# Where weight slabs and the tiles multiplied with them begin in SBUF, by remainder by 256 bytes

## The chip, the cores and the metric

The kernel runs on one core of a Trainium2 chip. The metric is the device time of one execution in microseconds; of several runs the median counts. The time before is 2227.2 us, the median of 3 runs (2226.93 to 2227.43).

## The reference

Two blocks follow each other on 256 tokens of width 1024, all in float32. The first block is one layer of attention with three branches, a pooling mixer and an MLP of width 4096 with a squared ReLU. The second block has two layers: sliding-window attention and a gated short convolution, each followed by a layer of experts. The experts take most of the time:

```python
def peer_ffn(xn, w_query, sub_keys, expert_u, expert_v):
    ...
    s_top, i_top = lax.top_k(s, PEER_TOPK)
    ...
    g = jax.nn.softmax(g_s, axis=-1)
    ...
        u = jnp.take(expert_u, ic, axis=0)
        a = jnp.einsum('td,thkd->thk', xc, u).astype(jnp.float32)
        w = (gc * jax.nn.gelu(a, approximate=False)).astype(xc.dtype)
        v = jnp.take(expert_v, ic, axis=0)
        return jnp.einsum('thk,thkd->td', w, v)
```

There are 16384 experts per layer. The kernel does not gather: it multiplies all tokens with all rows of `expert_u`, sets the weight of those that a token did not choose to zero, and multiplies with all rows of `expert_v`.

## The kernel before

**Slabs.** All weights come from HBM as 715 slabs of 128 partitions x 1024 float32 values (512 KB), in the order of one list, `plan`. The class `Stream` loads a slab into one of three raw places (`wraw`, a DMA on SP's queue), and then splits it: ScalarE rounds it to a high part `wh` (float32r, L70), and VectorE, or GpSimd for some slabs, subtracts to get the low part `wl` (L71). There are four places for `wh` and four for `wl`; slab j uses place j modulo 4 of each. `W.get()` gives the next slab and sees to it that the three after it are being split.

**Products.** The activations are kept in two parts too. A product is three matmuls into the same PSUM bank, written in `dense3`: high weights by high activations, high weights by low activations, low weights by high activations.

```python
        mm(out, h[:, s], xh[:, 0, k], first and opens, False)
        mm(out, h[:, s], xh[:, 1, k], False, False)
        mm(out, l[:, s], xh[:, 0, k], False, last)
```

All matmuls go through the helper `mm` (L174). In most stages (`tmode`) a block of the slab, 128 columns, is the weight operand that TensorE loads, and a tile of activations, 256 columns (one for each token), is the moving operand. These tiles are `xh` (two of them, used in turn by most stages), `mid` (the hidden values of the MLP, 4 tiles), `xo` and `oh` (attention outputs), `ph` and `mh` (pooling mixer) and `gA` (the convolution's tile takes this place). In the second half of each expert layer (`mix`) it is the other way round: a block of `xh` (the weighted activations) is the weight operand, and half of a slab part, 512 columns, is the moving operand; its results are in the banks named `g`. Two small products have narrow weights: `gh` (24 columns, blocks 96 bytes apart, by `xh`) and `movh` (30 columns, by slab parts).

**Order.** Each expert layer is written out in a manual order. While TensorE multiplies with `expert_u`, VectorE chooses the top 16 for each token and head (`topk`) and then builds one-hot tables, from which TensorE makes the gates (`gate`). Both are cut into pieces, and after each slab's matmuls some pieces follow, by fixed costs. The order of all instructions is therefore set when the program is built.

**Where tiles begin.** Tiles are taken from pools, and a pool hands out the bytes of a partition one after another. Where a tile begins follows from what was asked for ahead of it. A slice of a slab part that is loaded as weights begins at a multiple of 512 bytes from the part's start, and a moving slice of activations at a multiple of 1024, so each has the remainder by 256 of its tile.

Of the kernel before, what the change touches and what calls it, by code (L numbers as in the profile page):

```python
# [8 lines left out]
F32 = mybir.dt.float32  # L9
F32R = mybir.dt.float32r  # L10
# [8 lines left out]
P = 128  # L19
# [28 lines left out]
class Stream:  # L48
# [11 lines left out]
    def pump(self, i):  # L60
        nc, n = self.nc, len(self.plan)
        while True:
            if self.split < min(i + self.AHEAD + 1, n) and self.split < self.loaded:
                j = self.split
                self.split += 1
                r = self.raw.pop(j)
                h = self.pool.tile([P, 1024], F32R, name="wh", bufs=self.SPL)
                l = self.pool.tile([P, 1024], F32R, name="wl", bufs=self.SPL)
                for s in (slice(0, 1024),) if j else (slice(0, 512), slice(512, 1024)):
                    nc.scalar.copy(h[:, s], r[:, s])  # L70
                    (nc.gpsimd if j in self.pooled else nc.vector).tensor_sub(l[:, s], r[:, s], h[:, s].bitcast(F32))  # L71
                self.hl[j] = (h, l)
            elif self.loaded < n and self.loaded < self.split + self.RAW:
                self.load()
            else:
                return

    def load(self, half=None):

        if half != 1:  # L80
            self.raw[self.loaded] = self.pool.tile([P, 1024], F32, name="wraw", bufs=self.RAW)
            self.loaded += 1
        j = self.loaded - 1
        s = slice(0, 1024) if half is None else slice(512 * half, 512 * half + 512)
        self.nc.sync.dma_start(self.raw[j][:, s], self.plan[j][:, s])
# [21 lines left out]
def build(tc, a):  # L107
# [172 lines left out]
    xhp = ctx.enter_context(tc.tile_pool(name="xhp", bufs=1))  # L280

    def xh_tile(i):
        return xhp.tile([P, 2, KD, T], F32R, name=f"xh{i}")

    def sq_tile():
        return glob.tile([P, KD, T], F32, name="misc")
# [19 lines left out]
    bp = b1.enter_context(tc.tile_pool(name="b1", bufs=1))  # L306
    pa = b1.enter_context(tc.tile_pool(name="pa", bufs=1, space=PSUM))

    xh = xh_tile(0)
    sq = sq_tile()  # L310
    for i in range(0, KD, 2):
# [81 lines left out]
    for u in range(2):  # L393
        h, l = W.get()
# [24 lines left out]
    for c in range(2):  # L419
        for u in range(4):  # L420
            wh, wl = W.get()
# [229 lines left out]
    h, l = W.get()  # L651
# [54 lines left out]
    ff = ExitStack()  # L706
    fpool = ff.enter_context(tc.tile_pool(name="ff", bufs=1))
    pf = ff.enter_context(tc.tile_pool(name="pf", bufs=1, space=PSUM))
    mid = [fpool.tile([P, 2, KD, T], F32R, name=f"mid{i}") for i in range(4)]
    rel = [fpool.tile([P, 2, T], F32, name=f"rel{i}") for i in range(2)]  # L710
    sq2 = fpool.tile([P, 2, T], F32, name="sq2")
# [232 lines left out]
    for u in range(2):  # L944
        h, l = W.get()
# [552 lines left out]
```

## Time and profile before

| | us |
|---|---|
| median of 3 runs | 2227.2 |
| lowest and highest of them | 2226.93, 2227.43 |
| the profiled execution's own time | 2228.21 |
| its span, first to last instruction | 2226.4 |
| TensorE busy in the span | 2186.1 |
| VectorE busy | 1594.8 |
| ScalarE busy | 1084.5 |
| GpSimd busy | 148.2 |

The profile is of one execution. Matmuls are pipelined: the recorded duration of one is longer than the distance to the next, so durations in a row overlap, and the sum of a group's durations is more than the time it takes. The load of a matmul's weights is recorded as an instruction of its own (PEld), and runs beside the matmul ahead of it. L174 is the line of the helper, so groups are told apart by the names of their tiles: `mm<-xh,wh` is a matmul into a bank named mm with `xh` and `wh` as its two operands.

### The profile page before, as it was taken

To read this page: it belongs to the slowest core of one execution; us is meant where nothing else is said; L and a number is where in the kernel's file an instruction comes from. 1 tells how busy PE (TensorE), PEld (TensorE's weight loads), DVE (VectorE), ACT (ScalarE), POOL (GpSimd) and SP (SyncE) were. 2 spreads that over 40 slices of the span, in tenths; PEclk is the share of its full clock that TensorE was granted. 3 is DMA by queue.
4 is the path that set the end of the run, shared out by engine and by line. 5 is a ranking of instruction groups with operands and counts; after the bars stand their busy time and mean duration, and the time that the engine had idled before them with its cause. 6 is when DMAs were issued, how large, how long until landed. Compare 5 with 4: busy or idle time off the path is not lost.

```text
span 2226.4 us, 39574 instructions
## 1 busy us (share of the span) xinstructions
PE 2186.1 (98%) x15892; PEld 2040.8 (92%) x15892; DVE 1594.8 (72%) x2802; ACT 1084.5 (49%) x1707; POOL 148.2 (7%) x66
## 2 busy tenths in 40 slices
PE   8999999999989999999999999999899999999999
PEld 7899999999989999988888889999899999888887
DVE  7757656666998899755555566779988986555555
ACT  5555555564434444445454454544444435454454
POOL 0000000001442000000000000044300000000000
PEclk9999999999999999999999999999999999999999
DMA  6435555334544444455555555545444445555554
GB/s 208 152 133 180 181 190 190 105 134 151 189 143 167 152 161 157 164 196 190 197 190 196 191 172 180 191 164 174 154 150 162 152 147 195 197 191 196 191 190 150
DMA packets 105625, 382.67 MB, mean 172 GB/s; under 512 B 11985, under 2 KB 12385, under 8 KB 105185
## 3 DMA queue, kind: packets, MB, share of 16 engines
q1 hardware_dynamic: 105120, 378.04, 48.9%
q8 instruction: 124, 2.03, 0.4%
q0 software_dynamic: 320, 2.11, 0.3%
q14 instruction: 61, 0.49, 0.1%
HBM read 379.05 MB, written 1.05 MB: 171 GB/s over the span
## 4 chain that ended last, share of the span: by engine, by line
PE 84%; DVE 10%; issue 3%; ACT 2%; DMA 1%; SPq 0%; ACTq 0%; DVEq 0%
PE mm L174 46%; PE g L174 34%; DVE wl L71 3%; PE s L174 2%; DVE gA L1117 2%; ACT wh L70 1%; PE o L174 1%; DVE gA L1115 1%; DVE gA L1114 1%; DMA wraw<-in_w_in 0%; DVE gA L1197 0%; DVE lows L1178 0%; DVE misc L1179 0%; DMA x<-in_x 0%; DVE gA L1087 0%
## 5 line engine op out<-in xcount | busy, mean ns | idle before, releaser
L71 DVE TENSOR_TENSOR wl<-wraw,wh 128x1024 fp32r<-128x1024 f32 (+1 forms) x660 | 824.0, 1249 | 512.5 <-ACT wh L70 509.1
L174 PE MATMUL mm<-xh,wh 128*128 128x256 f32 x6240 | 1148.6, 286 | 9.1 <-ACT wh L70 6.9
L70 ACT CAST wh<-wraw 128x1024 fp32r<-128x1024 f32 (+1 forms) x716 | 747.0, 1054 | 726.3 <-PE g L174 332.6
L174 PEld LDWEIGHTS mm<-xh,wh 128*128 128x128 f32 x6240 | 979.9, 193 | 11.7 <-ACT wh L70 7.5
L174 PE MATMUL mm<-xh,wl 128*128 128x256 f32 x3120 | 889.1, 285 | 13.2 <-DVE wl L71 13.2
L174 PE MATMUL g<-wh,xh 128*128 128x512 f32 x2048 | 632.6, 389 | 0.0
L174 PEld LDWEIGHTS mm<-xh,wl 128*128 128x128 f32 x3120 | 602.4, 193 | 15.5 <-DVE wl L71 15.4
L174 PEld LDWEIGHTS g<-wh,xh 128*128 128x128 f32 x2048 | 384.4, 188 | 79.8
L174 PE MATMUL g<-wl,xh 128*128 128x512 f32 x1024 | 398.4, 389 | 0.0
L174 PEld LDWEIGHTS g<-wl,xh 128*128 128x128 f32 x1024 | 192.2, 188 | 39.5
L71 POOL TENSOR_TENSOR wl<-wraw,wh 128x1024 fp32r<-128x1024 f32 x56 | 142.7, 2547 | 285.2 <-ACT wh L70 271.5
L1199 ACT ACTIVATE gA<-g 128x96 f32<-128x96 f32 (+14 forms) x72 | 23.4, 343 | 243.8 <-DVE gA L1197 225.2
L1218 DVE TENSOR_TENSOR xh<-gA,xh 128x256 fp32r<-128x256 f32 x224 | 93.5, 418 | 0.0
L1217 ACT CAST xh<-gA 128x256 fp32r<-128x256 f32 x224 | 90.1, 403 | 0.0
L174 PE MATMUL mm<-mid,wh 128*128 128x256 f32 x512 | 87.1, 276 | 0.0
L1234 ACT ACTIVATE gA<-mm 128x512 f32<-128x512 f32 (+15 forms) x112 | 55.6, 496 | 63.4 <-PE mm L174 63.4
L174 PEld LDWEIGHTS mm<-mid,wh 128*128 128x128 f32 x512 | 77.0, 188 | 0.0
L174 PE MATMUL g<-misc 128*128 128x128 f16 x512 | 67.0, 221 | 9.9 <-DVE misc L1179 9.9
L174 PEld LDWEIGHTS <-misc 128*128 128x128 f16 x1024 | 59.8, 98 | 13.1 <-issue 6.8
L174 PE MATMUL mm<-mid,wl 128*128 128x256 f32 x256 | 70.7, 276 | 0.0
L174 PE MATMUL g<-lows,misc 128*128 128x128 f16 x512 | 66.4, 220 | 0.0
L1197 DVE SCALAR_TENSOR_TENSOR gA<-g,gA 128x512 f32<-128x512 f32 (+30 forms) x114 | 57.1, 538 | 0.0
(346 smaller groups left out, 1570.2 us busy)
## 6 DMA issues: line engine op xcount, KB each, us to landing
wraw<-in_peer_u SPq DMA_DIRECT2D x256, 512.0 KB, 3.5
wraw<-in_peer_v SPq DMA_DIRECT2D x256, 512.0 KB, 3.5
wraw<-in_w_ff SPq DMA_DIRECT2D x64, 512.0 KB, 4.4
wraw<-in_w_query SPq DMA_DIRECT2D x32, 512.0 KB, 3.6
wraw<-in_w_in SPq DMA_DIRECT2D x29, 512.0 KB, 4.0
wraw<-in_w_cin SPq DMA_DIRECT2D x24, 512.0 KB, 3.6
wraw<-in_w_qkv SPq DMA_DIRECT2D x12, 512.0 KB, 4.1
wraw<-in_w SPq DMA_DIRECT2D x8, 512.0 KB, 3.5
```

The costliest lines, as they stand in the source:

```text
L70: nc.scalar.copy(h[:, s], r[:, s])
L71: (nc.gpsimd if j in self.pooled else nc.vector).tensor_sub(l[:, s], r[:, s], h[:, s].bitcast(F32))
L174: PE.matmul(out, l, r, start=start, stop=stop, skip_group_check=True)
L1114: V.tensor_tensor(eq, pb, J[:, None].to_broadcast([P, 2, NCAND, 16]), op=OP.is_equal)
L1115: V.tensor_tensor(prod, eq, code[:, hq:hq + 2, :, None].to_broadcast([P, 2, NCAND, 16]), op=OP.mult)
L1117: V.reduce_sum(sel[:, hq:hq + 2], prod.rearrange("p h c k -> p h k c"), axis=AX.X)
L1197: V.scalar_tensor_tensor(v, pr[:, i0:j], 2.0 ** -15, v, op0=OP.mult, op1=OP.mult)
L1199: S.activation(d[:, j - i0:i1 - i0, t0:t0 + 8], pr[:, j:i1], AF.Copy, scale=2.0 ** -15)
L1217: S.copy(w[0], gA(e))
L1218: V.tensor_sub(w[1], gA(e), w[0].bitcast(F32))
L1234: S.activation(d[:, :, n:], ps[:, :, n:], AF.Gelu)
```

## The change

The change moves tiles by inserting small unused ones. Ahead of the first tile of each of the eight places of slab parts 32 bytes are taken, and the eight places become tiles with names of their own (`wh0`, `wl0`, `wh1` and so on), each used by every fourth slab, as before. Ahead of `xh` 32 bytes are taken, and ahead of `mid` 64.

```diff
-                h = self.pool.tile([P, 1024], F32R, name="wh", bufs=self.SPL)
-                l = self.pool.tile([P, 1024], F32R, name="wl", bufs=self.SPL)
+                h, l = self.place("wh", j), self.place("wl", j)
...
+    def place(self, name, j):
+
+        name = f"{name}{j % self.SPL}"
+        if j < self.SPL:
+            self.pool.tile([P, 8], F32, name="gap" + name)
+        return self.pool.tile([P, 1024], F32R, name=name)
...
+    xhp.tile([P, 8], F32, name="gap")
     xh = xh_tile(0)
...
+    fpool.tile([P, 16], F32, name="gap3")
     mid = [fpool.tile([P, 2, KD, T], F32R, name=f"mid{i}") for i in range(4)]
```

In the two built programs the tiles begin at these bytes of a partition (remainder by 256 behind each):

| tile | before | after |
|---|---|---|
| `wh`, four places | 35808, 39904, 44000, 48096 (all 224) | 35840 (0), 44096 (64), 52352 (128), 60608 (192) |
| `wl`, four places | 52192, 56288, 60384, 64480 (all 224) | 39968 (32), 48224 (96), 56480 (160), 64736 (224) |
| `wraw`, three places | 13280, 17376, 21472 (all 224) | the same |
| `xh`, two tiles | 68576, 84960 (both 224) | 68864, 85248 (both 0) |
| `mid`, four tiles | 112544 and every 16384 after it (all 160) | 112896 and every 16384 after it (all 0) |
| `xo`, `gA` | 142048, 150240; 101856 (all 224) | 142336, 150528; 102144 (all 0) |
| `oh`, `ph`, `mh` | 148736, 177664, 185856 (all 0) | 149024, 177952, 186144 (all 32) |

The instructions of every engine, their order and what they wait for are the same in the two programs.

## Rows read from the trace of the kernel before

**Rows 1.** The page: busy time of each engine, share of the span, instructions.

```profile
PE 2186.1 (98%) x15892; PEld 2040.8 (92%) x15892; DVE 1594.8 (72%) x2802; ACT 1084.5 (49%) x1707; POOL 148.2 (7%) x66
```

**Rows 2.** The page: the chain that ended last, by engine and by line.

```profile
PE 84%; DVE 10%; issue 3%; ACT 2%; DMA 1%; SPq 0%; ACTq 0%; DVEq 0%
PE mm L174 46%; PE g L174 34%; DVE wl L71 3%; PE s L174 2%; DVE gA L1117 2%; ACT wh L70 1%; PE o L174 1%; DVE gA L1115 1%; DVE gA L1114 1%; DMA wraw<-in_w_in 0%; DVE gA L1197 0%; DVE lows L1178 0%; DVE misc L1179 0%; DMA x<-in_x 0%; DVE gA L1087 0%
```

**Rows 3.** Three stretches: PE, PEld, DVE, ACT, POOL busy us; clock, DMA share, GB/s.

```profile
600.00:707.00 107.00, 98.04 (x797) 97.28 (x797) 103.78 (x192) 44.87 (x52) 44.50 (x17) 0.97 0.45 157
707.00:886.00 179.00, 179.00 (x1687) 177.88 (x1687) 155.55 (x230) 79.67 (x163) 0.00 (x0) 0.99 0.45 158
1515.00:1622.00 107.00, 98.01 (x805) 97.22 (x804) 103.80 (x198) 45.40 (x53) 44.71 (x17) 0.98 0.46 158
```

**Rows 4.** The chain in order of time, three pieces: start, us, what, how many.

```profile
309.93 72.43 PE mm L174 x639
...
918.48 37.48 PE mm L174 x312
...
955.96 345.47 PE g L174 x1524
```

**Rows 5.** TensorE by shape, 918 to 955 us: count | busy us, mean ns.

```profile
L174 PE MATMUL mm<-xh,wh 128*128 128x256 f32 x204 | 36.8, 283 | 0.0
L174 PE MATMUL mm<-xh,wl 128*128 128x256 f32 x102 | 28.9, 283 | 0.0
```

**Rows 6.** TensorE by shape, 310 to 390 us.

```profile
L174 PE MATMUL mm<-mid,wh 128*128 128x256 f32 x426 | 72.5, 276 | 0.0
L174 PE MATMUL mm<-mid,wl 128*128 128x256 f32 x213 | 58.8, 276 | 0.0
```

**Rows 7.** TensorE by shape, 166 to 180 us.

```profile
L174 PE MATMUL mm<-oh,wh 128*128 128x256 f32 x64 | 11.4, 279 | 0.0
L174 PE MATMUL mm<-oh,wl 128*128 128x256 f32 x32 | 9.0, 281 | 0.0
```

**Rows 8.** Groups by shape, whole run: matmuls (PE) and weight loads (PEld).

```profile
L174 PE MATMUL mm<-xh,wh 128*128 128x256 f32 x6240 | 1148.6, 286 | 9.1 <-ACT wh L70 6.9 <-ACT gA L1234 0.7 <-ACT xh L195 0.6
L174 PEld LDWEIGHTS mm<-xh,wh 128*128 128x128 f32 x6240 | 979.9, 193 | 11.7 <-ACT wh L70 7.5 <-ACT xh L195 0.9 <-DVE xh L196 0.9
L174 PE MATMUL mm<-xh,wl 128*128 128x256 f32 x3120 | 889.1, 285 | 13.2 <-DVE wl L71 13.2
L174 PE MATMUL g<-wh,xh 128*128 128x512 f32 x2048 | 632.6, 389 | 0.0
L174 PE MATMUL g<-wl,xh 128*128 128x512 f32 x1024 | 398.4, 389 | 0.0
L174 PE MATMUL mm<-mid,wh 128*128 128x256 f32 x512 | 87.1, 276 | 0.0
L174 PEld LDWEIGHTS mm<-mid,wh 128*128 128x128 f32 x512 | 77.0, 188 | 0.0
L174 PE MATMUL mm<-mid,wl 128*128 128x256 f32 x256 | 70.7, 276 | 0.0
```

**Rows 9.** TensorE by shape, 600 to 707 us, then 1515 to 1622 us.

```profile
L174 PE MATMUL mm<-xh,wh 128*128 128x256 f32 x518 | 95.7, 287 | 0.0
L174 PE MATMUL mm<-xh,wl 128*128 128x256 f32 x259 | 74.6, 288 | 5.7 <-DVE wl L71 5.7
...
L174 PE MATMUL mm<-xh,wh 128*128 128x256 f32 x523 | 96.2, 286 | 0.0
L174 PE MATMUL mm<-xh,wl 128*128 128x256 f32 x262 | 75.3, 287 | 5.6 <-DVE wl L71 5.6
```

**Rows 10.** The tiles gh and movh: count, duration ns min/median/max, first and last start.

```profile
L174 PE MATMUL mm<-xh,gh x24: 276/278/679, 45.7 to 48.8; 128*24 128x256 f32 x24
...
L174 PE MATMUL o<-wh,movh x64: 276/277/284, 48.9 to 59.7; 128*30 128x256 f32 x64
```

**Rows 11.** TensorE by shape, 955.7 to 957.3 us.

```profile
L174 PE MATMUL g<-wh,xh 128*128 128x512 f32 x5 | 1.6, 392 | 0.0
```

## The prediction

> **What bounds the kernel.** I read the page's busy times first, then the chain of waits, then a table by stage, then the groups of TensorE by shape. TensorE is busy in 98% of the span [rows 1], and the chain that ended last lies on it for 84%, on the matmuls of slab parts above all [rows 2]. Two places are different: while the top-k runs in each of the two expert layers (600 to 707 us and 1515 to 1622 us), VectorE is busy in 103.78 of 107 us and TensorE waits for it [rows 3]. In the stretch after it, 707 to 886 us, VectorE has 155.55 of 179 us [rows 3], so it could follow a TensorE that is some per cent faster; the granted clock is 0.97 to 0.99 in all three. So the time is a number of matmuls times their distance from each other, outside of 2 x 107 us.
>
> **How a distance is read.** 312 matmuls of `xh` by slab parts take 37.48 us, which is 120.1 ns each; 639 of `mid` by slab parts take 72.43 us, 113.3 ns each; 1524 of 512 columns take 345.47 us, 226.7 ns each [rows 4]. In the same stretches the recorded durations are 283, 276 and 389 ns [rows 5, 6, 8]. Each is 163 ns more than the distance, so for matmuls in a row a duration less 163 is the distance. That lets single groups be read where the chain merges them.
>
> **The row that this change is about.** The 283 and the 276 belong to the same instruction: 128x128 weights, 256 moving columns, the same three products (high part twice, low part once) for each block. What differs is where the operands lie. With `xh` both operands have remainder 224 by 256; with `mid` the weights have 224 and the moving tile 160, a difference of +64. With `oh` (weights 224, moving 0, a difference of -32) the durations are 279 (high) and 281 (low), so (2x279+281)/3-163 = 117 ns [rows 7]. The load of the next weights is recorded beside the running matmul, and its own mean is 193 ns with `xh` and 188 ns with `mid` [rows 8]. So the distance seems to hang on where the weight load reads against the moving read: 120 at difference 0, 117 at -32, 113 at +64.
>
> **The change part by part.**
> 1. Instructions, DMAs, waits and their order: nothing is added, removed or moved on any queue. A place is used again by every fourth slab, as before, so no new wait arises. Cost 0.
> 2. The 256-column matmuls of `xh`. There are 6240 + 3120 = 9360 [rows 8]. Those in the two VectorE-bound stretches, 518+259+523+262 = 1562 [rows 9], gain nothing: there VectorE's work sets the pace. That leaves 7798. Before, all stand at difference 0. After, the slab parts stand at 0, 64, 128, 192 (high) and 32, 96, 160, 224 (low) against moving tiles at 0. The rows know three of these eight with full weights: 120, 113, 117. All eight occur in the small product with `gh` (24 columns of weights, blocks 96 bytes apart): durations from 276, median 278, so 115 ns; the product with `movh` (30 columns), at many more differences, has 276 to 284 and a median of 277, 114 ns [rows 10]. Short loads read less and should collide less. I take 116 ns, between those 115 and the mean of 120, 113 and 117. The ends are 113.3 (all clear) and 120 (none better); no row of steady matmuls is above that. Gain: 7798 x 4.0 ns = 31.2 us, ends 0 and 7798 x 6.7 = 52.2 us.
> 3. The 768 matmuls with `mid` (512 + 256) [rows 8] already stand at 113.3. Their tile moves to remainder 0 and meets the same mix as the others, 116: a loss of 768 x 2.7 = 2.1 us, ends 0 and 768 x 6.7 = 5.1.
> 4. The 512-column matmuls (2048 + 1024) [rows 8], where the slab part is the moving operand. Difference 0 before, the mix after. Two readings of 226.7. As 389-283 = 106 ns for 256 more columns, it could be those 120 and undisturbed columns after that; then the same 6.7 ns of collision is in it, and clear ones would be at 220. Or it is 2 x 113.3, as clear as `mid`, and can only get worse: right after the stage begins, five matmuls have a mean of 392, 3 ns more than later [rows 11], so these do settle into a better state. I weigh the first reading higher, since the weight load ends long before 512 columns have passed, and take half of its 4 ns: 3072 x 2.0 = 6.1 us gain; ends 3072 x 6.7 = 20.6 gain, and 3072 x 3 = 9.2 loss.
> 5. The few hundred with `xo`, `gA`, `oh`, `mh` and `ph` and the short ones: under 2 us in either direction, taken as 0.
> 6. The splits on ScalarE and VectorE read and write the moved places too. They are hidden: VectorE has 72% [rows 1] and its waits are not on the chain but for the two stretches. No row tells what a remainder does to them; I take 0, and 2% of the 208 us in the two stretches [rows 3], 4 us, as a bound both ways.
>
> Sum: 31.2 - 2.1 + 6.1 = 35.2 us gain. The profiled execution took 2228.2 us (span 2226.4), so 2193 for it. The median of the runs, 2227.2, is 1.0 below it, so I predict **2192 us**. What is late next: the split of slabs on VectorE in the 707 to 886 us stretch, still with a few per cent to spare, and the slab DMAs, whose engines have a busy share of 0.45 to 0.46 in these stretches [rows 3].
>
> **A rule that speaks against it.** The rows show 120 and 113 for one instruction. The Trainium skill, SBUF — State Buffer, section Who interferes with whom, gives TensorE two independent read ports, one for the moving operand and one for the weights, and says "PE and ACT never wait on anyone". By that rule the places would change nothing and the sum would be 0. The trace speaks against it with 283 beside 276, but each of the two belongs to its own stage, so it isn't settled; it is rival C.
>
> **The rivals.** (About 0.2%, 4.5 us, is what a measurement of this kernel can tell from no change.)
> - A, nearly everything clears: 256 columns at 114 or less, 512 columns near 220. 7798 x 6 + 3072 x 4 to all ends = 59 to 73 us gain, so 2154 to 2168. For: five of the eight differences are unseen with full weights, and the one at +64 is perfectly clear. Against: even with narrow weights, `gh` and `movh` have medians 1 and 2 ns above the clear 276 and single rows far above it [rows 10].
> - B, little clears: what matters is only that some difference exists which isn't +64; all go as `oh`, 117 to 118. 7798 x 2.2 = 17.2, less 768 x 4.5 = 3.5 for `mid`: 13.7 gain, about 2213.
> - C, no effect of places: `mid` is faster for a reason of its stage, and 2227 stays. Against: `oh` and `mh` are in the middle of stages with `xh`, with the same slabs, the same engines at work, and still differ.
> - D, slower: the 512-column matmuls lose the settled state. Place: both weighted sums, 3072 matmuls. Price: 3 ns each, 9.2 us, and 5.1 us for `mid` at 120. It decides when the 7798 gain less than 1.3 ns each (9.2+5.1-4.5 = 9.8 us over 7798). With 0.5 ns: 14.3 - 3.9 = 10.4 us slower, 2238. For: the rows at the stage's start are longer; at a difference that changes from slab to slab it could start anew each time. Against: short loads and `oh` show that 256-column matmuls gain at nearly every other difference.
>
> **Chances and range.** The forecast (2180 to 2205) 0.54, A 0.17, B 0.15, C 0.08, D 0.06. Faster by over 0.2%: 0.54+0.17+0.15 = 0.86. Within: 0.08. Slower: 0.06. The range leaves out D, C and the outer third of A, 0.06+0.08+0.06 = 0.20: from 2160 to 2222.
>
> **What would show it.** Right: the duration of `xh` by slab parts in the steady stretch falls from 283 to about 279, not evenly, but with a pattern that repeats every four slabs; `mid` rises from 276 to about 279; the two stretches of top-k keep their 107 us; the 512-column group is at or a little under 389. Wrong: all four places alike (then the difference isn't what counts), `mid` still at 276 (then the stage is what counts), the 512-column group over 389 (D), or a gain of TensorE that comes back as idle time before `wl` L71.

## The result, and the profile after

The changed kernel takes 2240.36 us in the median of 3 runs (2239.64 to 2240.98), against 2227.2 before: the ratio is 1.0059, 95% interval 1.0036 to 1.0082. It is 13 us slower, where 35 us faster was forecast. The profiled execution after took 2240.98 us, with a span of 2239.2.

First the page after: busy times, and the chain that ended last by engine and by line (L180 is now the line of the matmul helper, L69 and L70 the two splits).

```profile
PE 2192.3 (98%) x15892; PEld 2029.2 (91%) x15892; DVE 1595.0 (71%) x2802; ACT 1083.9 (48%) x1707; POOL 149.9 (7%) x66
...
PE 74%; DVE 15%; ACT 5%; issue 4%; DMA 2%; POOL 0%; SPq 0%; ACTq 0%; DVEq 0%
```

TensorE is still busy in 98% of the span, with the same number of instructions on every engine as in [rows 1]; its share of the chain went from 84% [rows 2] to 74%, VectorE's from 10 to 15.

Next the groups of TensorE by shape, whole run, after (count | busy us, mean ns | idle before).

```profile
L180 PE MATMUL mm<-xh,wh 128*128 128x256 f32 x6240 | 1132.4, 283 | 12.0 <-ACT wh L69 6.3 <-ACT gA L1242 4.3 <-DVE mh L202 0.5
L180 PE MATMUL mm<-xh,wl 128*128 128x256 f32 x3120 | 884.6, 284 | 15.4 <-DVE wl L70 15.1
L180 PE MATMUL g<-wh,xh 128*128 128x512 f32 x2048 | 641.8, 393 | 0.0
L180 PE MATMUL g<-wl,xh 128*128 128x512 f32 x1024 | 405.5, 396 | 0.0
L180 PE MATMUL mm<-mid,wh 128*128 128x256 f32 x512 | 90.8, 280 | 0.0
L180 PE MATMUL mm<-mid,wl 128*128 128x256 f32 x256 | 72.1, 281 | 0.0
```

Against [rows 8]: `xh` fell from 286 and 285 to 283 and 284, `mid` rose from 276 to 280 and 281, and the 512-column matmuls rose from 389 to 393 and 396. The chain in order of time says it in distances (start, us, what, how many):

```profile
917.92 36.90 PE mm L180 x312
954.82 353.69 PE g L180 x1524
```

The row of 312 `xh` matmuls is 0.58 us shorter than in [rows 4] (118.3 ns each for 120.1), the row of 1524 with 512 columns 8.22 us longer (232.1 for 226.7).

How single matmuls spread is seen in the view of one tile's instructions (count: duration ns min/median/max, first and last start). Before, 1100 to 1108 us:

```profile
L174 PE MATMUL g<-wh,xh x25: 389/389/389, 1099.8 to 1107.9; 128*128 128x512 f32 x25
L174 PE MATMUL g<-wl,xh x12: 389/389/389, 1100.2 to 1107.7; 128*128 128x512 f32 x12
```

and after, the same stretch:

```profile
L180 PE MATMUL g<-wh,xh x24: 388/393/398, 1099.9 to 1107.8; 128*128 128x512 f32 x24
L180 PE MATMUL g<-wl,xh x12: 390/398/401, 1099.7 to 1107.4; 128*128 128x512 f32 x12
```

Before, every one of them takes 389 ns; after, they take from 388 to 401, and 34 of the 36 take more than 389. The `xh` matmuls in 920 to 930 us spread likewise, around a lower median. Before, then after:

```profile
L174 PE MATMUL mm<-xh,wh x58: 283/283/283, 919.8 to 930.0; 128*128 128x256 f32 x58
L174 PE MATMUL mm<-xh,wl x28: 283/283/283, 920.0 to 929.8; 128*128 128x256 f32 x28
```

```profile
L180 PE MATMUL mm<-xh,wh x58: 276/280/286, 919.9 to 930.0; 128*128 128x256 f32 x58
L180 PE MATMUL mm<-xh,wl x29: 276/281/286, 919.8 to 929.7; 128*128 128x256 f32 x29
```

**Where the 13 us came from.** The two programs issue the same 15,892 matmuls in the same order, so each can be paired with itself in the other trace, and the distance to the next start compared. "Without a wait" is a distance under 315 ns in both traces. Summed by kind, after less before:

| distances after | matmuls | us |
|---|---|---|
| 512 columns | 3071 | +16.4 |
| `mid` | 768 | +3.7 |
| `xh`, slab parts, outside the two top-k stretches, without a wait | 7783 | -12.8 |
| the two top-k stretches, waits and all | 1597 | +0.7 |
| everything else, without a wait | 2610 | +0.2 |
| waits outside of them | 62 | +4.7 |
| sum | 15891 | +12.9 |

The sum is the difference of the spans, 2239.2 less 2226.4. Per matmul that is -1.6 ns for `xh`, +4.8 for `mid`, +5.3 for 512 columns. Of the 7783 `xh` distances, 7561 are steady ones (under 140 ns in both traces), and their mean fell from 119.9 to 118.0 ns; the other 222, longer ones, took 1.7 us more. Two rows show where part of the `xh` gain came back. The top-k stretch did not move with TensorE (PE, PEld, DVE, ACT, POOL busy us; clock; DMA share; GB/s):

```profile
600.00:707.00 107.00, 95.92 (x799) 94.81 (x798) 103.86 (x192) 44.79 (x52) 44.77 (x17) 0.98 0.47 158
707.00:883.00 176.00, 176.00 (x1691) 174.90 (x1690) 152.62 (x226) 79.42 (x163) 0.00 (x0) 1.00 0.48 158
```

VectorE has 103.86 us of the 107, as in [rows 3], and TensorE idles 2 us more there. And in the gate stage TensorE now waits for ScalarE to empty the `mm` bank (engine, line waited for: us, times, longest), first before, then after:

```profile
PE mm L174 <- ACT gA L1234: 0.7, 1, 0.7
```

```profile
PE mm L180 <- ACT gA L1242: 4.3, 5, 1.2
```

All of the 4.7 us of waits in the table lie in the two gate stages, 885 to 920 and 1800 to 1836 us.

The granted clock is 0.98 and 1.00 in these stretches, 0.97 and 0.99 before [rows 3], so it does not make the time longer.

### The profile page after: what moved, and what is told of

Read it like the earlier page. It is cut to its first block, busy times and chain, and to the rows that moved or that the text cites. A ratio compares the mean times of both kernels' runs of the same rounds, so it can differ in the third digit from the quotient of the medians.

```text
span 2239.2 us, 39574 instructions
## 1 busy us (share of the span) xinstructions
PE 2192.3 (98%) x15892; PEld 2029.2 (91%) x15892; DVE 1595.0 (71%) x2802; ACT 1083.9 (48%) x1707; POOL 149.9 (7%) x66
## 4 chain that ended last, share of the span: by engine, by line
PE 74%; DVE 15%; ACT 5%; issue 4%; DMA 2%; POOL 0%; SPq 0%; ACTq 0%; DVEq 0%
PE mm L180 36%; PE g L180 34%; DVE wl L70 6%; ACT wh L69 3%; PE s L180 2%; PE o L180 2%; DVE gA L1125 1%; DMA wraw<-in_peer_u 1%; DVE gA L1205 1%; DVE lows L1186 1%; DVE gA L1122 1%; ACT act L1239 1%; DVE gA L1123 1%; ACT gA L1242 0%; DVE misc L1187 0%
## 5 line engine op out<-in xcount | busy, mean ns | idle before, releaser
L70 DVE TENSOR_TENSOR wl<-wraw,wh 128x1024 fp32r<-128x1024 f32 (+1 forms) x660 | 825.3, 1251 | 528.5 <-ACT wh L69 526.8
L180 PE MATMUL mm<-xh,wh 128*128 128x256 f32 x6240 | 1132.4, 283 | 12.0 <-ACT wh L69 6.3
L69 ACT CAST wh<-wraw 128x1024 fp32r<-128x1024 f32 (+1 forms) x716 | 745.6, 1052 | 743.0 <-PE g L180 349.1
L180 PEld LDWEIGHTS mm<-xh,wh 128*128 128x128 f32 x6240 | 966.3, 190 | 15.4 <-ACT wh L69 6.8
L180 PE MATMUL mm<-xh,wl 128*128 128x256 f32 x3120 | 884.6, 284 | 15.4 <-DVE wl L70 15.1
L180 PE MATMUL g<-wh,xh 128*128 128x512 f32 x2048 | 641.8, 393 | 0.0
L180 PEld LDWEIGHTS mm<-xh,wl 128*128 128x128 f32 x3120 | 591.8, 190 | 18.1 <-DVE wl L70 18.1
L180 PEld LDWEIGHTS g<-wh,xh 128*128 128x128 f32 x2048 | 384.9, 188 | 91.6
L180 PE MATMUL g<-wl,xh 128*128 128x512 f32 x1024 | 405.5, 396 | 0.0
L180 PEld LDWEIGHTS g<-wl,xh 128*128 128x128 f32 x1024 | 192.1, 188 | 43.7
L70 POOL TENSOR_TENSOR wl<-wraw,wh 128x1024 fp32r<-128x1024 f32 x56 | 144.3, 2576 | 281.1 <-ACT wh L69 269.2
L180 PE MATMUL mm<-mid,wh 128*128 128x256 f32 x512 | 90.8, 280 | 0.0
L180 PE MATMUL g<-misc 128*128 128x128 f16 x512 | 68.6, 223 | 10.5 <-DVE misc L1187 10.5
L180 PEld LDWEIGHTS mm<-mid,wh 128*128 128x128 f32 x512 | 78.6, 188 | 0.0
L180 PEld LDWEIGHTS <-misc 128*128 128x128 f16 x1024 | 61.3, 99 | 13.6 <-issue 7.1
L180 PE MATMUL mm<-mid,wl 128*128 128x256 f32 x256 | 72.1, 281 | 0.0
L180 PE MATMUL g<-lows,misc 128*128 128x128 f16 x512 | 67.7, 223 | 0.0
```

The source lines that it names most:

```text
L180: PE.matmul(out, l, r, start=start, stop=stop, skip_group_check=True)
```

## The experiments

Three theories were set against each other.

- Theory 1: what counts is the difference by 256 between the start of the weights and the start of the moving operand. While it stays the same along a row of matmuls, the row settles into a pattern that repeats; where it changes, the pattern is broken and has to form again. One difference may have more than one pattern.
- Theory 2: each difference has a fixed mean price, and the order in which they come is of no matter.
- Theory 3: the absolute place of a tile counts.

Remainders and differences below are in bytes; a difference is weights less moving, so the same tiles have +64 in the 256-column matmuls and -64 (192) in the 512-column ones, where they change roles. Distances are from start to start in the trace, of matmuls without a wait between them. The lists of medians, and the means by difference, are worked out from these starts.

### One difference everywhere: +64

On the kernel before, `xh`, `mid`, `xo` and `gA` all begin at remainder 160, slab parts at 224.

```diff
+    xhp.tile([P, 48], F32, name="gap")
     xh = xh_tile(0)
...
+    fpool.tile([P, 16], F32, name="gap3")
     mid = [fpool.tile([P, 2, KD, T], F32R, name=f"mid{i}") for i in range(4)]
```

> The kernel before with the activations (both xh, mid, xo, gA) at remainder 160 and all slab parts left at 224: one difference, +64, everywhere, the one at which mid stood before. Theory 1 (what counts is the difference of weights and moving operand, and that it stays the same from one matmul to the next, so that the two reads settle): xh by slab parts falls from 283 to 276 ns, 6.7 ns x 7798 = 52 us; the 512-column matmuls settle at 389 or below; together 2175 us or less. Theory 2 (each difference has its own cost, whatever stands next to it): 256 columns at +64 cost what they cost in the changed kernel, 118 ns, a gain of 2 x 7798 = 15.6 us, and 512 columns at -64 some 4.5 ns more than before, a loss of 13.8 us: about 2225 us. Theory 3 (what counts is where the slab parts themselves lie, next to what the other engines write): they have not moved, 2227 us.

Measured: 2226.66 us (2220.16 to 2239.89, 10 runs) against 2228.83 (13 runs), ratio on record 0.9999 (0.9979 to 1.0018): no difference is shown. Two large terms cancel: in the profiled execution the steady `xh` matmuls gained 28.4 us and the 512-column ones, now at -64, lost 18.9; 8.4 us came back as waits. Theory 1's forecast of 2175 us is missed by 50: the 512-column matmuls rose to 397 ns where it had 389 or below, and only a part of the `xh` matmuls went to 276 ns. Theory 2's 2225 us is met, but by luck: both of its terms (15.6 and 13.8 us) were too small, and the errors cancel.

But +64 is not one price. The tile view of `xh` in 540 to 545 us and then in 920 to 930 us of one execution, both at +64:

```profile
L174 PE MATMUL mm<-xh,wh x32: 276/276/276, 539.8 to 545.0; 128*128 128x256 f32 x32
L174 PE MATMUL mm<-xh,wl x15: 276/276/276, 540.0 to 544.8; 128*128 128x256 f32 x15
...
L174 PE MATMUL mm<-xh,wh x58: 281/281/281, 919.9 to 929.9; 128*128 128x256 f32 x58
L174 PE MATMUL mm<-xh,wl x29: 281/281/281, 919.8 to 929.7; 128*128 128x256 f32 x29
```

Both are perfectly steady: distances of 113, 113, 114 in the one row, of 118, 117, 118 in the other. A row takes one of the two near its beginning and keeps it until a wait or another shape ends it: of the 130 unbroken rows of `xh` and `mid` in this trace that are longer than eight matmuls, none changes its pattern after the sixth. About half of their matmuls have the shorter one. So a difference does not fix a price, which is against Theory 2. The runs of this kernel also spread over 20 us, those of before beside them over 9; that the two patterns make this spread is likely, but one of the ten executions alone was traced.

### High and low part of a place alike

On the change: `wh` and `wl` of a place share a remainder, 0, 64, 128 or 192; all 24 (12 with 512 columns) matmuls of a slab then have one difference.

```diff
-        if j < self.SPL:
-            self.pool.tile([P, 8], F32, name="gap" + name)
+        if j < self.SPL and name[1] == "h":
+            self.pool.tile([P, 16 if j else 8], F32, name="gap" + name)
...
-    xhp.tile([P, 8], F32, name="gap")
+    xhp.tile([P, 16], F32, name="gap")
```

> The changed kernel, but the high and the low part of one place share a remainder: 0, 64, 128, 192 for the four places; the activations stay at 0. So the difference is the same for the 24 or 12 matmuls of one slab and changes from slab to slab. Theory 1: after a few matmuls each slab settles; every fourth slab (place 1, +64) is at 113 ns and place 0 at 120 ns, as before; 512 columns at place 0 are at 226.7 ns; the whole is faster than the changed kernel's 2240 by 10 us or more. Theory 2: the same mean as in the changed kernel, 118 ns and 231.7 ns, 2240 +- 5 us. Theory 3: as the changed kernel, 2240.

Measured: 2240.89 us, one run (before on this chip: 2223.88 to 2232.74). That is Theory 2's time; the gain of 10 us that Theory 1 forecast did not come. The view of the 512-column tile, 1100 to 1108 us:

```profile
L180 PE MATMUL g<-wh,xh x24: 388/394/404, 1100.0 to 1107.8; 128*128 128x512 f32 x24
L180 PE MATMUL g<-wl,xh x12: 389/394/397, 1099.7 to 1107.4; 128*128 128x512 f32 x12
```

Within a slab one now sees the pattern form. The medians of the distances by position in a slab (512 columns, difference 0, 64 slabs):

```
226 236 228 233 231 227 227 227 227 227 227 227
```

Five matmuls after the slab's difference has changed, the 226.7 of the kernel before is there again; the next slab breaks it. At difference +64 the slab settles too, and after one matmul, but at 233. So for 512 columns 0 is the good difference, and the change gave it up in seven places of eight. It also shows that the starts count by 256 and not by 512: by the gaps asked for, the first slab part and `xh` begin 33024 bytes apart here, 129 times 256, and 32768 before, 128 times 256, and both have 226.7 (here at the first place, once the pattern has formed). The 256-column matmuls: 120 at 0 (a third of the slabs repeat 124, 117, 118, 121, 120 instead), 115 at +64 (a mix of 113.3 and 117.7), 118.4 at 128, 116.7 at 192 (again 113.3 and 117.7).

### The four differences between

The same with 32, 96, 160, 224 (16 floats ahead of each `wh`, none changed ahead of `xh`).

```diff
-        if j < self.SPL:
-            self.pool.tile([P, 8], F32, name="gap" + name)
+        if j < self.SPL and name[1] == "h":
+            self.pool.tile([P, 16], F32, name="gap" + name)
```

> As the run before, with the four places at 32, 96, 160 and 224. Theory 1: place 3 (224, that is -32) repeats 119, 116, 118 ns, as oh did before; every place shows a short pattern of its own that repeats within the slab; faster than 2240 by 10 us or more. Theory 2: 2240 +- 5 us with a spread of patterns as in the changed kernel. Theory 3: 2240.

Measured: 2246.72 us, one run, where Theory 1 forecast 2230 or less and Theory 2 up to 2245. 256 columns: 118.4 at 32, 118.5 at 96, 120.0 (high) and 119.1 (low) at 160, 116.7 at 224. 512 columns: 233.3 to 235.7 by place and part, mean 233.6. None of the four is good for either shape.

With this the change can be reckoned again. Two of three of its matmuls use the high part, which has the differences of the second experiment, and one the low part, which has those of this one. For 256 columns the means of the two experiments, 117.6 and 118.3, give (2 x 117.6 + 118.3) / 3 = 117.8, and the change has 118.0 in its steady rows. For 512 columns 231.1 and 233.6 give 231.9, and the change has 232.1. So for both shapes the mean over differences was the right way to reckon, and to this extent Theory 2 holds; for `xh` the value was 118, not 116.

### All places moved, no difference changed

On the kernel before, 32 bytes ahead of the first slab part; everything behind moves with it.

```diff
+                if not j:
+                    self.pool.tile([P, 8], F32, name="gap")
                 h = self.pool.tile([P, 1024], F32R, name="wh", bufs=self.SPL)
```

> The kernel before with one gap of 32 bytes ahead of all slab parts: slab parts and xh at remainder 0, mid at 192, every difference as before (0 for xh, +64 for mid, -32 for oh), every place 32 bytes further. Theories 1 and 2: 2227 +- 4 us, 283, 276 and 389 ns as before. Theory 3: another time, by more than 5 us, since all places have moved against the raw slabs.

Measured: 2226.72 us, one run, and the groups of before to the nanosecond for 512 columns and `mid`:

```profile
L176 PE MATMUL g<-wh,xh 128*128 128x512 f32 x2048 | 632.5, 389 | 0.0
L176 PE MATMUL g<-wl,xh 128*128 128x512 f32 x1024 | 398.4, 389 | 0.0
L176 PE MATMUL mm<-mid,wh 128*128 128x256 f32 x512 | 87.1, 276 | 0.0
```

(L176 is the helper's line in this kernel.) Here the slab parts and `xh` begin at remainder 0, not 224, and `mid` at 192. The time and the groups stay, so Theory 3 falls.

### +64 for 256 columns, 0 for 512

The first experiment, with the weighted activations of the expert layers' second half written 64 bytes further, so that their difference from the slab parts is 0 again.

```diff
+        def slot(p, e):
+            o = 256 * (e % 4) + 16
+            return h[:, p].rearrange("p k t -> p (k t)")[:, o:o + T]
...
-            w = h[:, 0, e % 4], h[:, 1, e % 4]
+            w = slot(0, e), slot(1, e)
...
-            wh, wl = (h[:, p, e % 4, t * P:(t + 1) * P] for p in range(2))
+            wh, wl = (slot(p, e)[:, t * P:(t + 1) * P] for p in range(2))
```

> The kernel with all activations at +64 (run e1_all64), but the weighted activations of the second half of the expert layers are written 64 bytes further into their tile, so that there, and there alone, the difference is 0 again. Theory 1, as it stands after that run (a constant difference lets a row of matmuls settle into a pattern; +64 with 256 columns has two, 113.3 and 117.7 ns, the start of the row decides; 512 columns settle at 226.7 with difference 0 and at 233 with -64): the 512-column groups go from 396 back to 389 ns, 6.1 ns x 3072 = 18.8 us less than e1_all64, about 2207 us, faster than both kernels by 20 us or more. Theory 2 (a mean cost for each difference, no settling) gives the same here. If the second half were slow in e1_all64 for another reason (its tile's place, say), 2226 us would stay.

Measured: **2207.1 us** (2203.33 to 2214.17, 4 runs) against 2228.18 (7 runs), ratio 0.990 (0.9883 to 0.9917): 1% less than the kernel before, clear of the noise. The forecast was about 2207; that the median meets it so closely is in part luck, since the four runs spread over 11 us. In the chain the row of 1524 is back at its length of before, and the groups at 389:

```profile
949.38 345.47 PE g L174 x1524
```

```profile
L174 PE MATMUL g<-wh,xh 128*128 128x512 f32 x2048 | 632.5, 389 | 0.0
L174 PE MATMUL g<-wl,xh 128*128 128x512 f32 x1024 | 398.3, 389 | 0.0
```

The profiled execution is the slowest of the four (2214.17): steady `xh` -22.0 us, 512 columns 0.0, `mid` +3.4, and 6.5 us that came back as waits. About a fifth of its `xh` and `mid` matmuls have the shorter pattern, where the trace of the first experiment had half. `mid` lies at +64 here as it does before and in the first experiment. Its tile view in the first experiment (320 to 372 us), then here (320 to 380 us):

```profile
L174 PE MATMUL mm<-mid,wh x307: 276/276/276, 319.8 to 371.8; 128*128 128x256 f32 x154
L174 PE MATMUL mm<-mid,wl x154: 276/276/276, 319.9 to 372.0; 128*128 128x256 f32 x154
```

```profile
L174 PE MATMUL mm<-mid,wh x339: 281/281/281, 319.7 to 379.5; 128*128 128x256 f32 x170
L174 PE MATMUL mm<-mid,wl x170: 281/281/281, 319.9 to 379.6; 128*128 128x256 f32 x170
```

Up to there the two programs have the same instructions at the same places, and differ only in the expert layers behind. One execution took the 113.3 pattern, the other the 117.7, for the whole of the stage.

### Places close to +64

On the change: differences of 48, 56, 72 and 80, one for both parts of a place; the activations stay at 0.

```diff
+        o = (12, 14, 18, 20)[j % self.SPL]
         name = f"{name}{j % self.SPL}"
...
-        return self.pool.tile([P, 1024], F32R, name=name)
+        return self.pool.tile([P, 1088], F32R, name=name)[:, o:o + 1024]
```

> High and low part of the four places at 48, 56, 72 and 80, activations at 0: does a difference near +64 have only the clear pattern? Theory 1: rows of equal durations within each slab; of the four places at least one is at 113.3 in nearly all slabs if the two patterns at +64 hang on a few bytes; if they hang on the start of the row alone, all four show both, means of 115 to 118. The 512-column matmuls, at 176 to 208, have 231 to 234 and cost 15 us against before. About 2235 us.

Measured: 2241.18 us, one run, 6 more than forecast. 256 columns: 118.0 at 48, 117.8 at 56, 118.4 at 72, 118.6 at 80; 512 columns 230.6 to 236.1 by place and part, mean 233.0. No place has rows at 113.3. In the second experiment, where the difference also changes from slab to slab, slabs at +64 had a mean of about 115; eight bytes beside it little of that is left.

### The 512-column matmuls alone

On the kernel before, only the weighted activations of the second half move, by 192 bytes: difference -64 there, as in the first experiment, everything else as before.

```diff
+        def slot(p, e):
+            o = 256 * (e % 4) + 48
+            return h[:, p].rearrange("p k t -> p (k t)")[:, o:o + T]
...
```

> The kernel before, but the weighted activations of the second half of the expert layers lie 192 bytes further, difference -64 there, and all else as before. It prices the 512-column term by itself. Theory 1 and 2: 389 becomes 396 ns, 6.2 ns x 3072 = 19.0 us, 2247 us, and no other group changes. If 512-column matmuls did not depend on the difference: 2228 us.

Measured: 2236.34 us, one run, against a median of 2228.18: about 8 us slower, and of the 8.3 us that pairing finds between the profiled executions 6.7 are in the 512-column matmuls. Both theories had forecast 2247. The same difference cost 18.9 us in the first experiment. Its groups and, under them, those of the first experiment:

```profile
L174 PE MATMUL g<-wh,xh 128*128 128x512 f32 x2048 | 636.3, 391 | 0.0
L174 PE MATMUL g<-wl,xh 128*128 128x512 f32 x1024 | 401.5, 392 | 0.0
```

```profile
L174 PE MATMUL g<-wh,xh 128*128 128x512 f32 x2048 | 646.9, 397 | 0.0
L174 PE MATMUL g<-wl,xh 128*128 128x512 f32 x1024 | 406.1, 397 | 0.0
```

In the row of 1524 the distances repeat 226, 229, 232 here and 233, 233, 234 there: -64 has two patterns with 512 columns as well, and the loss is a third of the other run's at the same difference. In the first experiment itself the two long rows (1524 and 1218 matmuls) have the second pattern, and the four short ones near the end (48, 48, 48 and 179) have the first. So this run settles the sign of the term, not its size.

### Difference 0 that follows the slab's place

On the second experiment: the weighted activations follow the remainder of the place that their slab will have, so all 512-column matmuls have difference 0, but both operands jump by 64 from slab to slab.

```diff
+        vbase.append(len(plan))
         units("peer_v", 128 * l, 128 * l + 128)
...
+        def slot(p, e):
+            o = 320 * (e % 4) + 16 * ((vbase[l] + e) % 4)
+            return h[:, p].rearrange("p k t -> p (k t)")[:, o:o + T]
...
```

> Run e2_pair64 (places at 0, 64, 128, 192, high and low alike), but each weighted activation is shifted by the remainder of the slab that it will meet, so that in the second half of the expert layers the difference is 0 for every slab while the slabs' places still change. Theory 1: 389 ns throughout, 4.1 ns x 3072 = 12.6 us less than e2_pair64, 2228 us. If a change of the absolute place from slab to slab unsettled the row too: 392 or more, 2235 us or more.

Measured: 2238.02 us, one run, 2.9 less than the second experiment; Theory 1 forecast 2228, and 2235 or more was expected if a jump of the places unsettled the row too. The tile view, 1100 to 1108 us (L182 is the helper's line here):

```profile
L182 PE MATMUL g<-wh,xh x24: 388/394/398, 1099.8 to 1107.6; 128*128 128x512 f32 x24
L182 PE MATMUL g<-wl,xh x12: 387/389/390, 1100.3 to 1107.9; 128*128 128x512 f32 x12
```

By position in a slab the medians are

```
228 229 233 236 224 231 236 228 232 231 227 226
```

with a mean of 230.1. All differences are 0, yet the pattern is broken at each slab, and only the last two of the twelve are at 227 and 226. So a price by difference alone (Theory 2) does not hold for 512 columns, and Theory 1 has to be widened: a jump of both operands breaks a row as well as a change of difference does. One thing remains open here: the load of a matmul's weights runs beside the matmul ahead of it, so at each jump one load stands 64 bytes off from the slab that is still being read. Whether this one, or the jump itself, breaks the row, no run tells. Of the arrangements tried, only those in which neither operand jumps stay at 226.7.

## Why the prediction was wrong

Two steps failed: in item 4 the reading of 226.7 ns as a distance with a collision in it, which gave the 512-column matmuls a gain where they lost 16.4 us, and in item 2 the size of the gain for `xh`, taken from products with narrow weights. By items: the forecast was 35.2 us of gain, the trace shows 12.9 of loss, so 48.1 us are to be found.

- Item 1 held: the same instructions on every engine, and no new dependence.
- Item 2, `xh`, had the right sign and was mis-sized: 116 ns was taken and 118.0 measured in steady rows, a gain of 12.8 us for 31.2 (18.4 of the 48.1; 1.7 of them are longer distances, outside of the steady rows). The step that failed is the choice of the nearest row. The products with `gh` and `movh` [rows 10] have 24 and 30 columns of weights and stay at 115 to 117 ns in every run looked at; they say nothing of full weights. `oh` [rows 7], full weights at another difference, was the nearer row: by its starts it is at 117.8, not the 117 worked out from durations, and the seven differences other than +64 have a mean of 118.4. The 113 of `mid` was read as the price of +64; the first experiment and the one with 2207 us show that it is the better of two patterns there.
- Item 3, `mid`: a loss of 3.7 us for 2.1, for the same reason (4.8 ns and not 2.7). Within its ends.
- Item 4, 512 columns: the sign was wrong, +16.4 us for -6.1 (22.5 of the 48.1). Of the two readings of 226.7 the first was taken, "120 and undisturbed columns". The second, "as clear as `mid`, and can only get worse", is what the runs show: in none of the nine other kernels traced are the 512-column matmuls faster than 226.7 on average, and the one that restores difference 0 in a steady row has 226.7 again. The row that said so was in hand: the first five matmuls of the stage are slower than the rest [rows 11], which is the pattern forming. The end for this item was also too small: 3 ns were taken from that row, 5.3 came. Most of the 5.3 is the price of the other differences, as the reckoning behind the third experiment shows (231.9 for 232.1); breaking the pattern costs less, 1.6 ns a matmul at difference 0 in the second experiment (228.3 for 226.7).
- Item 5: 0.2 us without waits. It held.
- Item 6, the splits: the mean of a split on VectorE is 1251 ns after, and was 1249 before; nothing shows a price of places there, and the top-k stretches took 0.7 us more in all, inside its 4 us.
- Not in the sum: 4.7 us of waits outside the top-k stretches. What the prediction named as late next was the split on VectorE and the DMAs; ScalarE's reading of the `mm` bank in the gate stages was the one that came instead.

The rivals. B's price for `xh` (117 to 118) was right: it had 13.7 us of gain with `mid`, and 9.1 came. But it left the 512 columns alone. D named the mechanism and the place: "the 512-column matmuls lose the settled state", "at a difference that changes from slab to slab it could start anew each time". Its point of decision, a gain under 1.3 ns for each of the 7798, was too low only because its price was: with 5.3 ns and 4.8 ns the loss is 20.1 us, and 1.6 ns of gain do not cover it. That its example, 2238 us, lies near the 2240 measured is luck: its loss and its gain were both too small. The sign that the prediction gave for it, the 512-column group over 389, came. It had 0.06 of chance, and the measured time lies outside the range, which left it out.

C, no effect, is refuted from both sides: -1.6, +4.8 and +5.3 ns in three kinds of matmul by nothing but places. The Trainium skill (SBUF — State Buffer, Who interferes with whom) has TensorE's two reads on independent ports and waiting for no one. The measurement decides: the experiment that moves only the weights of the 512-column matmuls changes their distance from 226.7 to 228.9 ns. It does not tell whether the ports are what the two reads share.

**What is shown and what is open.** Shown: by how much the starts of the two operands differ, by 256, decides which distances a row of matmuls can have; a steady row settles into a short pattern that repeats; changing the difference breaks it for one to five matmuls, and in the one run with a jump of both starts it took ten; a difference can have two patterns, and two rows or two executions can take different ones. Only argued: that it is the load of the next weights that meets the moving read; no run here takes the load away. The recorded loads do not decide it. For `xh` they went with the distance, 193 ns before [rows 8] and 190 after, but for the 512-column matmuls they stayed at 188 while the distance rose by 5.3 ns. Before, then after:

```profile
L174 PEld LDWEIGHTS g<-wh,xh 128*128 128x128 f32 x2048 | 384.4, 188 | 79.8
```

```profile
L180 PEld LDWEIGHTS g<-wh,xh 128*128 128x128 f32 x2048 | 384.9, 188 | 91.6
```

Open: what makes a row take the one pattern or the other. A kernel that always took the better one at +64 would have the 113.3 of `mid` for `xh` too.

## What to carry to other kernels

Where TensorE sets the time, the byte at which a tile begins is a parameter: three shifts of 64 to 192 bytes were worth 1% here. Keep it the same for all buffers that a loop rotates through, set it per stage and shape (of the differences tried, 0 was best for 512 columns, +64 for 256), and do not spread buffers over remainders in the hope of an average: the average of eight was worse than the best in both shapes (118.0 where +64 everywhere had 116 to 117, and 232.1 where 0 had 226.7). Price such a change from steady rows of the same shape, and read slower instructions at the beginning of a stage as a sign that the rest is in a state that can be lost.

## What the runs showed that was not expected

- One instruction at one difference has two stable distances: 113.3 and 117.7 ns with 256 columns at +64 and at 192, 228.9 and 233.3 ns with 512 columns at -64. Which one holds is settled near a row's start; it lasted through the stage of `mid` and through the 1524 matmuls of the weighted sum.
- A kernel's time can spread without any disturbance of its clock: 2220 to 2240 us with +64 everywhere (10 runs), at granted clocks of 0.99 to 1.00, where the change itself had 2239.64 to 2240.98 in its three runs. The two patterns are the likely reason.
- The good places are narrow: 8 bytes beside +64, 117.8 to 118.4 ns (one run).
- A jump that leaves the difference at 0 costs nearly as much as one that changes it: 230.1 against 231.1 ns as the mean of 512 columns, where a steady row has 226.7.
